# One decoder layer on one core: the tokens of the dilated branch as an even and an odd tile

## The chip, the cores and the metric

The kernel runs on one core of one Trainium2 chip. Its metric is the device time of one execution in microseconds (us); several runs are given by their median. The engines named below are TensorE (PE in the rows, its weight loads PEld), VectorE (DVE), ScalarE (ACT), GpSimd (POOL) and SyncE (SP), which issues most of the DMAs.

## What is computed

A decoder layer with 256 tokens and 2048 channels: `h` is the normalised, modulated input, `proj = h @ w_in` has 20032 columns, and two branches of attention follow, whose gated outputs are projected, merged and projected once more. The change concerns branch B, the dilated attention, with 8 heads of 128 in each of three groups. Every group has its own queries, keys and values, and the outputs of the groups are weighted by their softmax denominators, which equals one softmax over the keys of all three:

```python
DIL_GROUPS = ((128, 1), (512, 4), (2048, 16))      # window, dilation
def dilated_branch(qkv, positions):
    q = partial_rotary(qkv[:, :, 0], positions)     # 32 of the 128 channels of a head are rotated
    k = partial_rotary(qkv[:, :, 1], positions)
    for g, (window, dilation) in enumerate(DIL_GROUPS):
        o, lse = dilated_group_attention(q[:, :, g], k[:, :, g], v[:, :, g], window, dilation)
    wts = jax.nn.softmax(jnp.stack(lses, axis=0), axis=0)
    o = jnp.sum(wts[..., None] * jnp.stack(outs, axis=0), axis=0)
```

A query attends to keys that are not later than itself: in the first group to those at most 128 tokens back, in the second to those whose distance is a multiple of 4, in the third to those whose distance is a multiple of 16.

## The kernel before

**Products with weights.** `load_split` fetches two blocks of 128 rows and 512 columns of a weight, and splits them into a rounded part (`whi`, a cast on ScalarE, L251) and the rest (`wlo`, a subtraction on VectorE, L252). `multiply` then issues 12 matmuls on L262: `hTh` with `whi`, `hTl` with `whi`, `hTh` with `wlo`, each for two blocks of rows and two tiles of 128 tokens. The stationary operand is a 128x128 block of the transposed activations (`Opd.get`), the moving one 512 columns of the weight. For `kva`, the keys' low-rank part, the columns are 256 and 320.

**Stages.** The head of the program alternates the modulation (`ada`, L193) with visits to 16 groups of columns (`head`): nine blocks of queries, keys and values of the dilated heads 0 to 3 (`d...0`), two of the gate `zd`, two of `kva`, three of the heads 4 to 7. In the last round of visits `rotary_tables` is called, and after the visit to `zd0` the rotation of the dilated queries and keys (`dil_rope`) and their attention (`dil_steps(0)`). Six more groups for heads 4 to 7 follow, then `dil_steps(1)`, the latent branch, and the output side.

**Steps beside the products.** Attention is cut into small steps in the list `side`; `run` takes one (`tick`) after each chunk of a product, so that they stand between chunks of 12 matmuls on TensorE. For one dilated head they are: `s1`, transposes of queries and keys into `qk`; `s2`, the scores, one tile of queries after the other, 128 keys for the first tile and 256 for the second in each of three groups, with masked maximum and exponential (`softmax`); `s3`, transposes of the probabilities, nine blocks (`probs_t`); `s4`, nine products with the values, and the gate. A pool framework orders the instructions of every engine; each engine works through its own queue in order. Matmuls on plain float32 operands, such as `s_D` and `pv_D`, leave two records each in the trace; transposes and the products of L262 leave one.

Lines of before that the rows name: L251 and L252 the split, L262 the products, L390 to L399 the angles, L412 and L413 the tables read with a step of two, L421 to L424 the rotation, L474 the masked maximum, L487 the transposes of `s3`, L495 and L496 those of `s1`, L525 the scores, L543 the products with the values, L636 the adding up of a visit's product in SBUF.

Of the kernel before, what the change touches and what calls it, by code (L numbers as in the profile page):

```python
# [49 lines left out]
T_MD0 = T_ZER + P  # L50
T_MD1 = T_MD0 + 3 * P
T_END = T_MD1 + 3 * S


def constant_table():
# [5 lines left out]
    rel0 = np.arange(P)[:, None] - np.arange(P)[None, :]  # L61
    rel1 = P + np.arange(P)[:, None] - np.arange(S)[None, :]

    def masks(rel):
        causal = rel >= 0
        return [causal & (rel <= 128), causal & (rel % 4 == 0), causal & (rel % 16 == 0)]

    t[:, T_MD0:T_MD0 + 3 * P] = np.where(np.concatenate(masks(rel0), 1), 0.0, NEG)
    t[:, T_MD1:T_MD1 + 3 * S] = np.where(np.concatenate(masks(rel1), 1), 0.0, NEG)
# [4 lines left out]
def hybrid_block(ctx: ExitStack, tc: tile.TileContext, x, c, positions, w_ada, b_ada, g_pre, g_post,  # L74
# [225 lines left out]
    for q in range(4):  # L300
# [8 lines left out]
        for t in range(2):  # L309
            j = sp.tile([P, 768], F32, tag="sm", name=f"junk_x{q}{t}")  # L310
# [64 lines left out]
    def rotary_tables():  # L375
        nc.sync.dma_start(msk, table[:, T_ZER:T_END])
        posi = cp.tile([2, P], I32, tag="posi", name="posi")
        nc.sync.dma_start(posi, positions[0].rearrange("(r p) -> r p", p=P))
# [25 lines left out]
        for h in range(2):  # L404
            for d in range(2):
                V.tensor_copy(cosM[:, :, h, d * 32:(d + 1) * 32], cs)
                V.tensor_scalar(sinM[:, :, h, d * 32:(d + 1) * 32], sn, 2.0 * d - 1.0, None, op0=ALU.mult)
        cs2 = cs.rearrange("p t (i two) -> p t i two", two=2)[:, :, :, 0]
        sn2 = sn.rearrange("p t (i two) -> p t i two", two=2)[:, :, :, 0]
# [72 lines left out]
    def probs_t(sm, nb, name):  # L482
        pT = sp.tile([P, 6, P], F32, tag="pT", name=f"pT_{name}")
        for b0 in range(0, nb, 3):
            pt = tp_tile([P, 3, P], f"pt_p{name}{b0}")
            for b in range(3):
                T.transpose(pt[:, b, :], sm[:, (b0 + b) * P:(b0 + b + 1) * P], ident)  # L487
            A.copy(pT[:, b0:b0 + 3, :], pt)
        return pT
# [396 lines left out]
```

## Time and profile before

| | |
|---|---|
| median of 3 runs (lowest to highest) | 1280.65 us (1280.48 to 1281.94) |
| profiled execution, its own time | 1281.44 us |
| its span, first to last instruction | 1279.7 us |
| TensorE busy | 1260.7 us, 99% of the span, 6101 matmul records |
| TensorE's weight loads busy | 1050.0 us, 82% |
| VectorE, ScalarE busy | 814.8 us (64%), 601.9 us (47%) |
| moved by DMA | 275.01 MB, 215 GB/s in the mean |

Busy time of an engine is the time in which one of its instructions is under way. Matmuls are pipelined: a record lasts longer than the distance to the next one. What a matmul takes on the path is therefore the distance of starts, and where many follow one another this is read from the starts of two groups in the timeline.

### The profile page before, as it was taken

What the parts mean: (1) busy time and instruction counts of PE and PEld (TensorE: products, weight loads), DVE (VectorE), ACT (ScalarE), POOL (GpSimd) and SP (SyncE); (2) the same over time, 40 slices, a digit from 0 to 9 for tenths busy, and PEclk for the clock granted to TensorE, in tenths of its full rate; (3) what the DMA queues carried; (4) which work ended last, traced back from release to release, by engine and by line L of the source; (5) the groups of instructions that cost most, each with busy time, mean ns of one, the idle gap of its engine ahead of it and who ended that gap; (6) DMA issues with size and microseconds to landing.
All of it is one profiled execution on the core that took longest, in us unless ns stands there. A gap on an engine that the chain in (4) does not pass through costs nothing.

```text
span 1279.7 us, 16445 instructions
## 1 busy us (share of the span) xinstructions
PE 1260.7 (99%) x6101; PEld 1050.0 (82%) x6101; DVE 814.8 (64%) x1201; ACT 601.9 (47%) x778; POOL 0.2 (0%) x4
## 2 busy tenths in 40 slices
PE   7999999999999999999999999999999999999997
PEld 3788888888888888888888888888888888888886
DVE  4878887897984645556566576664544444565545
ACT  3556334433374544464554555555544444434442
POOL 0000000000000000000000000000000000000000
PEclk9999999999999999999999999999999999999999
DMA  9999988987554566656577585775566666666741
GB/s 329 313 304 334 317 277 281 309 269 233 171 160 119 156 190 195 185 158 215 164 223 243 171 281 175 225 229 161 154 196 196 192 191 196 206 214 187 256 155 67
DMA packets 158172, 275.01 MB, mean 215 GB/s; under 512 B 9542, under 2 KB 46860, under 8 KB 158092
## 3 DMA queue, kind: packets, MB, share of 16 engines
q1 hardware_dynamic: 156276, 268.43, 67.9%
q10 hardware_dynamic: 1816, 5.53, 1.2%
q8 instruction: 48, 0.79, 0.2%
q14 instruction: 32, 0.26, 0.1%
HBM read 271.83 MB, written 2.10 MB: 214 GB/s over the span
## 4 chain that ended last, share of the span: by engine, by line
PE 98%; DVE 1%; DMA 0%; ACT 0%; issue 0%; DVEq 0%; SPq 0%; ACTq 0%
PE acc_d L262 31%; PE acc_mq L262 10%; PE acc_zm L262 7%; PE acc_gd L262 7%; PE acc_ym L262 7%; PE acc_gm L262 7%; PE acc_o L262 6%; PE acc_kv L262 3%; PE acc_yd L262 3%; PE acc_zd L262 3%; PE acc_kva L262 2%; PE pv_D L543 1%; PE s_D L525 1%; PE s_M L722 1%; PE row L186 1%; PE pt_pD L487 1%
## 5 line engine op out<-in xcount | busy, mean ns | idle before, releaser
L251 ACT CAST whi_d<-raw_d 128x1024 fp32r<-128x1024 f32 (+1 forms) x156 | 152.7, 986 | 182.5 <-PE acc_d L262 138.7
L252 DVE TENSOR_TENSOR wlo_d<-raw_d,whi_d 128x1024 fp32r<-128x1024 f32 (+1 forms) x156 | 176.4, 1139 | 72.6 <-ACT whi_d L251 70.9
L262 PE MATMUL acc_d<-whi_d,hTh 128*128 128x512 f32 x576 | 160.2, 396 | 1.4 <-DVE d L636 1.4
L262 PE MATMUL acc_d<-whi_d,hTl 128*128 128x512 f32 x576 | 157.2, 391 | 0.0
L262 PE MATMUL acc_d<-wlo_d,hTh 128*128 128x512 f32 x576 | 156.2, 390 | 0.0
L262 PEld LDWEIGHTS acc_d<-whi_d,hTl 128*128 128x128 f32 x576 | 108.5, 189 | 23.8 <-DVE hTl L229 0.8
L262 PEld LDWEIGHTS acc_d<-wlo_d,hTh 128*128 128x128 f32 x576 | 108.4, 188 | 22.9
L262 PEld LDWEIGHTS acc_d<-whi_d,hTh 128*128 128x128 f32 x576 | 106.3, 188 | 22.7 <-issue 1.8
L252 DVE TENSOR_TENSOR wlo_mq<-raw_mq,whi_mq 128x1024 fp32r<-128x1024 f32 x48 | 58.7, 1223 | 49.4 <-ACT whi_mq L251 44.6
L193 DVE SCALAR_TENSOR_TENSOR ada<-raw_a,ccol,ada 128x512 f32<-128x512 f32 (+1 forms) x96 | 77.4, 807 | 17.1 <-DMA raw_a<-in_w_ada 16.0
L251 ACT CAST whi_mq<-raw_mq 128x1024 fp32r<-128x1024 f32 x48 | 50.4, 1050 | 59.6 <-PE acc_mq L262 26.9
L252 DVE TENSOR_TENSOR wlo_gm<-raw_gm,whi_gm 128x1024 fp32r<-128x1024 f32 x32 | 39.2, 1225 | 45.4 <-ACT whi_gm L251 45.4
L252 DVE TENSOR_TENSOR wlo_gd<-raw_gd,whi_gd 128x1024 fp32r<-128x1024 f32 x32 | 39.2, 1224 | 37.3 <-ACT whi_gd L251 37.3
L252 DVE TENSOR_TENSOR wlo_zm<-raw_zm,whi_zm 128x1024 fp32r<-128x1024 f32 x32 | 39.2, 1224 | 33.5 <-ACT whi_zm L251 27.5
L252 DVE TENSOR_TENSOR wlo_ym<-raw_ym,whi_ym 128x1024 fp32r<-128x1024 f32 x32 | 39.1, 1222 | 32.1 <-ACT whi_ym L251 32.1
L251 ACT CAST whi_ym<-raw_ym 128x1024 fp32r<-128x1024 f32 x32 | 33.7, 1055 | 51.0 <-PE acc_ym L262 41.0
L251 ACT CAST whi_gm<-raw_gm 128x1024 fp32r<-128x1024 f32 x32 | 33.8, 1055 | 49.6 <-PE acc_gm L262 43.9
L252 DVE TENSOR_TENSOR wlo_o<-raw_o,whi_o 128x1024 fp32r<-128x1024 f32 x28 | 34.2, 1224 | 35.4 <-ACT whi_o L251 32.4
L262 PE MATMUL acc_mq<-whi_mq,hTh 128*128 128x512 f32 x192 | 55.2, 409 | 0.0
L251 ACT CAST whi_gd<-raw_gd 128x1024 fp32r<-128x1024 f32 x32 | 33.6, 1051 | 40.9 <-PE acc_gd L262 18.7
L251 ACT CAST whi_zm<-raw_zm 128x1024 fp32r<-128x1024 f32 x32 | 33.6, 1051 | 39.5 <-PE acc_zm L262 12.5
L262 PE MATMUL acc_mq<-whi_mq,hTl 128*128 128x512 f32 x192 | 51.6, 391 | 0.0
(279 smaller groups left out, 2352.2 us busy)
## 6 DMA issues: line engine op xcount, KB each, us to landing
raw_d<-in_w_in SPq DMA_DIRECT2D x132, 512.0 KB, 4.5
raw_mq<-in_w_in SPq DMA_DIRECT2D x48, 512.0 KB, 4.5
raw_a<-in_w_ada SPq DMA_DIRECT2D x80, 256.0 KB, 4.7
raw_zm<-in_w_in SPq DMA_DIRECT2D x32, 512.0 KB, 4.2
raw_g<-in_w_ada SPq DMA_DIRECT2D x32, 512.0 KB, 4.4
raw_gd<-in_w_in SPq DMA_DIRECT2D x32, 512.0 KB, 4.4
raw_gm<-in_w_in SPq DMA_DIRECT2D x32, 512.0 KB, 4.4
raw_ym<-in_w_mla_proj SPq DMA_DIRECT2D x32, 512.0 KB, 3.9
```

The lines of the kernel that those rows point to most:

```text
L186: T.matmul(row[0:1, j, 0:n], ccol[:, kk:kk + 1], v[:, k, j, :], start=kk == ROW_K[0], stop=kk == ROW_K[-1])
L193: V.scalar_tensor_tensor(flat, w, ccol[:, kk:kk + 1], flat, op0=ALU.mult, op1=ALU.add)
L251: A.copy(whi[:, :m], raw[:, :m])
L252: V.tensor_tensor(wlo[:, :m], raw[:, :m], whi[:, :m].bitcast(F32), ALU.subtract)
L262: T.matmul(acc[:, t, :n], opd.get(part, k0 + k, t), wt[:, k * n:(k + 1) * n], start=start and ph == 0 and k == 0, stop=stop and ph == 2 an ...
L487: T.transpose(pt[:, b, :], sm[:, (b0 + b) * P:(b0 + b + 1) * P], ident)
L525: T.matmul(sc[:, i * nk:(i + 1) * nk], qk[g][:, 0, t * P:(t + 1) * P], qk[g][:, 1, 0:nk], start=True, stop=True)
L543: T.matmul(pv, pT[:, b, :], dil[2, g, quad][:, kt, hs], start=b == 0, stop=b == nb - 1)
L722: T.matmul(sc[:, o:o + nk], qk[:, 0, t * P:(t + 1) * P], qk[:, 1, 0:nk], start=True, stop=False)
```

## The change

Tokens of the dilated branch are held as two tiles, the even tokens and the odd ones, instead of the first 128 and the last 128. A distance of 4 or 16 joins only tokens of the same tile, so groups 1 and 2 need one block of 128 keys for each tile of queries; group 0 needs both blocks in either tile. Per head the scores go from three products of 128 keys and three of 256 to two of 256 and four of 128; blocks of probabilities to transpose and to multiply with the values go from nine to eight.

To get there, the products for all dilated columns and for `zd` read `hT` through `hD`: the 128 columns of the stationary operand lie two elements apart. `kva` keeps `hT`. The rotary tables are made for four rows of positions (two in the old order for the latent branch, two even and odd), with a second small DMA that gathers the positions with a step of two. The gated output is written back in the order of tokens, by splits of 128 columns with a step of two. Masks and scratch tiles change their sizes; `sm` goes from two buffers of 768 columns to three of 512.

```diff
+    class OpdDil(Opd):
+        def get(self, part, k, t):
+            return part[k // 4][:, k % 4, :].rearrange("p (m t) -> p t m", t=2)[:, t]
+
     hT = Opd(hT_h, hT_l)
+    hD = OpdDil(hT_h, hT_l)
...
-        posi = cp.tile([2, P], I32, tag="posi", name="posi")
-        nc.sync.dma_start(posi, positions[0].rearrange("(r p) -> r p", p=P))
+        posi = cp.tile([4, P], I32, tag="posi", name="posi")
+        nc.sync.dma_start(posi[0:2], positions[0].rearrange("(r p) -> r p", p=P))
+        nc.sync.dma_start(posi[2:4], positions[0].rearrange("(m t) -> t m", t=2))
...
-        for t in range(2):
+        for t in range(4):
             V.tensor_scalar(ang[:, t, :], frq, posc[:, t:t + 1], None, op0=ALU.mult)
...
-            v = pt.rearrange("p b t n -> p b (t n)")
-            split(dst_h[i][:, 2 * hp:2 * hp + 2, :], dst_l[i][:, 2 * hp:2 * hp + 2, :], v)
+            if dilated:
+                for b in range(2):
+                    hi, lo = [d[i][:, 2 * hp + b, :].rearrange("p (m t) -> p t m", t=2)
+                              for d in (dst_h, dst_l)]
+                    split(hi, lo, pt[:, b])
...
+                sc = tp_tile([P, 4 * P], f"s_D{quad}{h}{t}")
+                own = slice(t * P, (t + 1) * P)
+                T.matmul(sc[:, 0:S], qk[0][:, 0, own], qk[0][:, 1, :], start=True, stop=True)
+                for g in (1, 2):
+                    T.matmul(sc[:, (g + 1) * P:(g + 2) * P], qk[g][:, 0, own], qk[g][:, 1, own],
+                             start=True, stop=True)
+                res.append(softmax(sc, md[t], SC_DIL, f"D{quad}{h}{t}"))
...
-                for b in range(nb):
-                    g, kt = divmod(b, t + 1)
-                    T.matmul(pv, pT[:, b, :], dil[2, g, quad][:, kt, hs], start=b == 0, stop=b == nb - 1)
+                for b, (g, kt) in enumerate(((0, 0), (0, 1), (1, t), (2, t))):
+                    T.matmul(pv, pT[:, b, :], dil[2, g, quad][:, kt, hs], start=b == 0, stop=b == 3)
...
-        run(acc, hT, win, a, upto, c0, n, nm)
+        run(acc, hT if nm.startswith("kva") else hD, win, a, upto, c0, n, nm)
...
-            acc = group(hT, win, KC, dil_col(s, g, 1), 512, nm)
+            acc = group(hD, win, KC, dil_col(s, g, 1), 512, nm)
```

TensorE's queue where the probabilities of the first head are turned (`pt_pD`, step `s3`) and the scores of the second are made (`s_D`, step `s2`); `acc_d` is the product that goes on between them. Before:

```order
L487 MATMUL pt_pD_3281<-tid,sm_D_3200 128x128 x3
L487 MATMUL pt_pD_3287<-tid,sm_D_3211 128x128 x3
L487 MATMUL pt_pD_3292<-tid,sm_D_3211 128x128 x3
L262 MATMUL acc_d_12_3298<-whi_d_12_3301,hTh_2277 128x512 x4
L262 MATMUL acc_d_12_3298<-whi_d_12_3301,hTl_2278 128x512 x4
L262 MATMUL acc_d_12_3298<-wlo_d_12_3302,hTh_2277 128x512 x4
L525 MATMUL s_D_3317<-qkD_3244 128x128
L525 MATMUL s_D_3317<-qkD_3251 128x128
L525 MATMUL s_D_3317<-qkD_3258 128x128
L525 MATMUL s_D_3327<-qkD_3244 128x256
L525 MATMUL s_D_3327<-qkD_3251 128x256
L525 MATMUL s_D_3330<-qkD_3258 128x256
```

The same place now:

```order
L502 MATMUL pt_pD_3282<-tid,sm_D_3203 128x128 x4
L502 MATMUL pt_pD_3289<-tid,sm_D_3213 128x128 x4
L274 MATMUL acc_d_12_3296<-whi_d_12_3299,hTh_2277 128x512 x4
L274 MATMUL acc_d_12_3296<-whi_d_12_3299,hTl_2278 128x512 x4
L274 MATMUL acc_d_12_3296<-wlo_d_12_3300,hTh_2277 128x512 x4
L536 MATMUL s_D_3315<-qkD_3245 128x256
L538 MATMUL s_D_3315<-qkD_3252 128x128
L538 MATMUL s_D_3315<-qkD_3259 128x128
L536 MATMUL s_D_3325<-qkD_3245 128x256
L538 MATMUL s_D_3325<-qkD_3252 128x128
L538 MATMUL s_D_3325<-qkD_3259 128x128
```

One transpose of nine is gone, and one of the three scores against 256 keys has become one against 128; the products around them stand as they stood.

TensorE's queue at the first head, where the rotated queries and keys are turned for the first time (`pt_qkD`, step `s1`; `d_203` and `d_206` are queries and keys of group 1, `d_204` and `d_207` those of group 2) between the products of `kva` and `zd`. Before:

```order
L262 MATMUL acc_kva_14_3177<-whi_kva_14_3180,hTh_2277 128x320 x2
L496 MATMUL pt_qkD_3162<-tid,d_206 128x128
L495 MATMUL pt_qkD_3162<-tid,d_203 128x128
L496 MATMUL pt_qkD_3162<-tid,d_206 128x128
L262 MATMUL acc_kva_14_3177<-whi_kva_14_3180,hTh_2277 128x320 x2
L262 MATMUL acc_kva_14_3177<-whi_kva_14_3180,hTl_2278 128x320 x4
L262 MATMUL acc_kva_14_3177<-wlo_kva_14_3181,hTh_2277 128x320 x4
L525 MATMUL s_D_3196<-qkD_3160 128x128
L525 MATMUL s_D_3196<-qkD_3167 128x128
L525 MATMUL s_D_3206<-qkD_3160 128x256
L525 MATMUL s_D_3206<-qkD_3167 128x256
L496 MATMUL pt_qkD_3169<-tid,d_207 128x128
```

The same place now, after four matmuls of `acc_kva` on `hTh`:

```order
L274 MATMUL acc_kva_14_3180<-whi_kva_14_3183,hTl_2278 128x320 x3
L511 MATMUL pt_qkD_3165<-tid,d_206 128x128
L510 MATMUL pt_qkD_3165<-tid,d_203 128x128
L511 MATMUL pt_qkD_3165<-tid,d_206 128x128
L274 MATMUL acc_kva_14_3180<-whi_kva_14_3183,hTl_2278 128x320
L274 MATMUL acc_kva_14_3180<-wlo_kva_14_3184,hTh_2277 128x320 x4
L536 MATMUL s_D_3199<-qkD_3163 128x256
L538 MATMUL s_D_3199<-qkD_3170 128x128
L536 MATMUL s_D_3209<-qkD_3163 128x256
L538 MATMUL s_D_3209<-qkD_3170 128x128
L274 MATMUL acc_zd_14_3221<-whi_zd_14_3224,hTh_2277 128x512 x2
L511 MATMUL pt_qkD_3172<-tid,d_207 128x128
```

The transposes of `d_206` stand five matmuls of `kva` later than they did, those of `d_207` two matmuls of `zd` later.

VectorE's queue at the same place: the rotation of `d_206` and `d_207` (its last step writes `d_206<-rt_d`) between the splits (`wlo`) and the adding up of visits (`zd`, `kva`). Before:

```order
L252 TENSOR_TENSOR wlo_zd_14_3224<-raw_zd_14_3221,whi_zd_14_3223 128x1024
L636 TENSOR_TENSOR zd_211<-zd_211,acc_zd_14_3079 128x1024
L424 TENSOR_TENSOR d_206<-rt_d_3124,rt_d_3125 128x8x32
L636 TENSOR_TENSOR kva<-kva,acc_kva_14_3136 128x2x256
L421 TENSOR_TENSOR rt_d_3130<-d_207,cosD 128x256
L422 TENSOR_TENSOR rt_d_3131<-d_207,sinD 128x8x16
L423 TENSOR_TENSOR rt_d_3131<-d_207,sinD 128x8x16
L252 TENSOR_TENSOR wlo_d_14_3265<-raw_d_14_3262,whi_d_14_3264 128x1024
L424 TENSOR_TENSOR d_207<-rt_d_3130,rt_d_3131 128x8x32
L636 TENSOR_TENSOR kva<-kva,acc_kva_14_3177 128x2x256
```

The same place now:

```order
L264 TENSOR_TENSOR wlo_zd_14_3225<-raw_zd_14_3222,whi_zd_14_3224 128x1024
L646 TENSOR_TENSOR zd_211<-zd_211,acc_zd_14_3082 128x1024
L435 TENSOR_TENSOR rt_d_3127<-d_206,cosD 128x256
L436 TENSOR_TENSOR rt_d_3128<-d_206,sinD 128x8x16
L437 TENSOR_TENSOR rt_d_3128<-d_206,sinD 128x8x16
L646 TENSOR_TENSOR kva<-kva,acc_kva_14_3139 128x2x256
L438 TENSOR_TENSOR d_206<-rt_d_3127,rt_d_3128 128x8x32
L264 TENSOR_TENSOR wlo_d_14_3266<-raw_d_14_3263,whi_d_14_3265 128x1024
L435 TENSOR_TENSOR rt_d_3133<-d_207,cosD 128x256
L436 TENSOR_TENSOR rt_d_3134<-d_207,sinD 128x8x16
L437 TENSOR_TENSOR rt_d_3134<-d_207,sinD 128x8x16
L646 TENSOR_TENSOR kva<-kva,acc_kva_14_3180 128x2x256
```

The last step of either rotation stands behind the adding up of `kva` that it stood ahead of (that of `d_207` is the row after the last one shown).

## Rows read from the trace of the kernel before

**Rows 1.** The page, chain of work that ended last, by engine:

```profile
PE 98%; DVE 1%; DMA 0%; ACT 0%; issue 0%; DVEq 0%; SPq 0%; ACTq 0%
```

**Rows 2.** Who waited for whom, TensorE: us in total, times, longest:

```profile
PE acc_d L262 <- DVE d L636: 1.4, 1, 1.4
```

**Rows 3.** Timeline of TensorE, dilated steps between chunks: start us, us from first start:

```profile
367.71 1.07 PE L262 MATMUL acc_d<-wlo_d,hTh 128*128 128x512 f32 x4
368.62 1.14 PE L487 MATMUL pt_pD<-tid,sm_D 128*128 128x128 f32 x9
...
370.53 1.08 PE L262 MATMUL acc_d<-whi_d,hTl 128*128 128x512 f32 x4
...
372.36 2.13 PE L525 MATMUL s_D<-qkD 128*128 128x128 f32 x12
...
375.25 1.08 PE L262 MATMUL acc_d<-whi_d,hTl 128*128 128x512 f32 x4
...
377.09 2.17 PE L543 MATMUL pv_D<-d,pT_D 128*128 128x128 f32 x18
...
380.02 1.08 PE L262 MATMUL acc_d<-whi_d,hTl 128*128 128x512 f32 x4
```

**Rows 4.** Groups by line and form, scores: busy us, mean ns | idle before:

```profile
L525 PE MATMUL s_D<-qkD 128*128 128x256 f32 x48 | 11.8, 380 | 0.0
...
L525 PE MATMUL s_D<-qkD 128*128 128x128 f32 x48 | 6.8, 274 | 0.0
```

**Rows 5.** Groups by line, TensorE's weight loads, same columns:

```profile
L262 PEld LDWEIGHTS acc_d<-whi_d,hTl 128*128 128x128 f32 x576 | 108.5, 189 | 23.8 <-DVE hTl L229 0.8
...
L186 PEld LDWEIGHTS row<-raw_a,ccol 128*1 128x1 f32 x36 | 2.8, 83 | 8.1 <-issue 7.2 <-DMA raw_a<-in_w_ada 0.9
```

**Rows 6.** Timeline of the weight loads, the first for the values' products:

```profile
376.86 1.31 PEld L543 LDWEIGHTS pv_D<-d,pT_D 128*128 128x128 f32 x10
```

**Rows 7.** Timeline of VectorE: start us, us, in brackets idle before and releaser:

```profile
328.37 1.23 DVE L252 TENSOR_TENSOR wlo_d<-raw_d,whi_d 128x1024 fp32r<-128x1024 f32 x1 [0.32 <-ACT whi_d L251]
...
330.91 1.22 DVE L636 TENSOR_TENSOR d<-d,acc_d 128x1024 f32<-128x1024 f32 x1 [0.20 <-PE acc_d L262]
...
333.10 0.17 DVE L412 COPY cosD<-cs 128x32 f32<-128x32 f32 x1
...
351.13 0.42 DVE L421 TENSOR_TENSOR rt_d<-d,cosD 128x256 f32<-128x256 f32 x1
...
357.08 0.42 DVE L424 TENSOR_TENSOR d<-rt_d,rt_d 128x256 f32<-128x256 f32 x1
357.42 0.68 DVE L636 TENSOR_TENSOR kva<-kva,acc_kva 128x512 f32<-128x512 f32 x1
...
359.89 0.42 DVE L424 TENSOR_TENSOR d<-rt_d,rt_d 128x256 f32<-128x256 f32 x1
```

**Rows 8.** Windows: us, busy of PE, PEld, DVE, ACT, POOL, clock, DMA share, GB/s:

```profile
331.00:363.00 32.00, 32.00 (x162) 27.24 (x161) 31.90 (x73) 13.59 (x18) 0.00 (x0) 1.00 0.58 172
363.00:420.00 57.00, 57.00 (x326) 49.36 (x325) 32.98 (x77) 34.69 (x55) 0.00 (x0) 1.00 0.47 132
```

**Rows 9.** Timeline of TensorE, first transposes of `d_206` and `d_207`, product of `kva`:

```profile
357.68 0.27 PE L496 MATMUL pt_qkD<-tid,d 128*128 128x128 f32 x1
...
358.30 0.75 PE L262 MATMUL acc_kva<-whi_kva,hTl 128*128 128x320 f32 x4
358.88 0.75 PE L262 MATMUL acc_kva<-wlo_kva,hTh 128*128 128x320 f32 x4
...
360.78 0.27 PE L496 MATMUL pt_qkD<-tid,d 128*128 128x128 f32 x1
```

**Rows 10.** Timeline of SyncE and VectorE, the positions' transfer and its first reader:

```profile
181.78 0.36 SPq L378 DMA_DIRECT2D posi<-in_positions  x1
...
189.70 0.21 DVE L380 CAST posf<-posi 2x128 f32<-2x128 int32 x1
...
194.11 0.75 DVE L193 SCALAR_TENSOR_TENSOR ada<-raw_a,ccol,ada 128x512 f32<-128x512 f32 x1 [2.73 <-DMA raw_a<-in_w_ada]
```

More of the change, by code (lines that the diff above doesn't have):

```diff
@@ L49, with dilated_tokens @@
 T_ZER = T_FRQ + 32
-T_MD0 = T_ZER + P
-T_MD1 = T_MD0 + 3 * P
-T_END = T_MD1 + 3 * S
+T_CAU = T_ZER + P
+T_MD = T_CAU + P
+T_END = T_MD + 2 * 4 * P
+def dilated_tokens(t):
+    return 2 * np.arange(P) + t
 def constant_table():
@@ L60, in constant_table @@
     t[:, T_FRQ:T_FRQ + 32] = inv.astype(np.float32)[None, :]
[L61 to L69, printed above, removed]
+    rel = np.arange(P)[:, None] - np.arange(P)[None, :]
+    t[:, T_CAU:T_CAU + P] = np.where(rel >= 0, 0.0, NEG)
+    for tile_q in range(2):
+        q = dilated_tokens(tile_q)[:, None]
+        rels = [q - dilated_tokens(tile_k)[None, :] for tile_k in (0, 1, tile_q, tile_q)]
+        ok = [(r >= 0) & (r <= 128) for r in rels[:2]]
+        ok += [(rels[2] >= 0) & (rels[2] % 4 == 0), (rels[3] >= 0) & (rels[3] % 16 == 0)]
+        c0 = T_MD + tile_q * 4 * P
+        t[:, c0:c0 + 4 * P] = np.where(np.concatenate(ok, 1), 0.0, NEG)
     return t
@@ L309, in hybrid_block @@
         for t in range(2):
-            j = sp.tile([P, 768], F32, tag="sm", name=f"junk_x{q}{t}")
+            j = sp.tile([P, 512], F32, tag="sm", bufs=3, name=f"junk_x{q}{t}")
             if t == 0:
@@ L405, in rotary_tables @@
             for d in range(2):
[L406 to L409, printed above, removed]
+                V.tensor_copy(cosM[:, :, h, d * 32:(d + 1) * 32], cs[:, 0:2])
+                V.tensor_scalar(sinM[:, :, h, d * 32:(d + 1) * 32], sn[:, 0:2], 2.0 * d - 1.0, None, op0=ALU.mult)
+        cs2 = cs[:, 2:4].rearrange("p t (i two) -> p t i two", two=2)[:, :, :, 0]
+        sn2 = sn[:, 2:4].rearrange("p t (i two) -> p t i two", two=2)[:, :, :, 0]
         for h in range(4):
@@ L450, in transpose_split, with transpose_steps @@
             split(hi[:, 2 * hp:2 * hp + 2, :], lo[:, 2 * hp:2 * hp + 2, :], v)
-    def transpose_steps(src, dst_h, dst_l, i, name):
+    def transpose_steps(src, dst_h, dst_l, i, name, dilated=False):
         def step(hp):
@@ L482, in probs_t @@
     def probs_t(sm, nb, name):
[L483 to L488, printed above, removed]
+        pT = sp.tile([P, 4, P], F32, tag="pT", bufs=2, name=f"pT_{name}")
+        pt = tp_tile([P, nb, P], f"pt_p{name}")
+        for b in range(nb):
+            T.transpose(pt[:, b, :], sm[:, b * P:(b + 1) * P], ident)
+        A.copy(pT[:, 0:nb, :], pt)
         return pT
@@ L499, in qk_t @@
         return qk.rearrange("p (a t) n -> p a (t n)", a=2)
-    md0 = msk[:, P:4 * P]
-    md1 = msk[:, 4 * P:4 * P + 3 * S]
+    md = [msk[:, (2 + 4 * t) * P:(6 + 4 * t) * P] for t in range(2)]
     mm = [msk[:, P:2 * P], msk[:, 0:2 * P]]
@@ L519, in s2 @@
             for t in range(2):
-                nk = (t + 1) * P
-                srcs = []
-                for gs in ((0, 1, 2),) if t == 0 else ((0, 1), (2,)):
-                    sc = tp_tile([P, len(gs) * nk], f"s_D{quad}{h}{t}{gs[0]}")
-                    for i, g in enumerate(gs):
-                        T.matmul(sc[:, i * nk:(i + 1) * nk], qk[g][:, 0, t * P:(t + 1) * P],
-                                 qk[g][:, 1, 0:nk], start=True, stop=True)
-                    srcs.append(sc)
-                res.append(softmax(srcs, md1 if t else md0, 3 * nk, SC_DIL, f"D{quad}{h}{t}"))
+                sc = tp_tile([P, 4 * P], f"s_D{quad}{h}{t}")
[5 more added lines that the diff above has]
+                res.append(softmax(sc, md[t], SC_DIL, f"D{quad}{h}{t}"))
             kept[h] = res
         def s3(h):
-            kept[h] = [(probs_t(sm, 3 * (t + 1), f"D{quad}{h}{t}"), rl) for t, (sm, rl) in enumerate(kept[h])]
+            kept[h] = [(probs_t(sm, 4, f"D{quad}{h}{t}"), rl) for t, (sm, rl) in enumerate(kept[h])]
         def s4(h):
@@ L548, in dil_steps @@
         return ([lambda f=f, h=h: f(h) for f, h in order]
-                + transpose_steps(lambda: bb[0], bbT_h, bbT_l, quad, "bb"))
+                + transpose_steps(lambda: bb[0], bbT_h, bbT_l, quad, "bb", True))
     ckv_h, ckv_l = [], []
```

37 lines of the change are left out of this document (17 added, 20 removed).

## Prediction

> **What bounds the kernel now.** Read the chain of work that ended last first: 98% of it is TensorE [rows 1]. Then ask whether TensorE ever waits in the steady state: the table of who waited for whom has one wait in a product of L262, 1.4 us once [rows 2]. So inside the products the time is what TensorE's queue takes, matmul after matmul, and an edit is worth what it takes out of that queue or puts into it. VectorE, ScalarE and the DMAs matter only where TensorE would come to wait for them.
>
> A record's duration is not that price, since matmuls overlap; the distance of starts is. Four matmuls of 512 columns start in 368.62 - 367.71 = 0.91 us, 0.2275 us each, at the full granted clock [rows 3, 8]. For the small pieces, take the distance between the group and the second group behind it, and take off the four matmuls of 0.91 us between (the first matmul behind a float32 group has its start put too early). Nine transposes: 370.53 - 368.62 - 0.91 = 1.00, 0.111 us each. Eighteen records of the values' products: 380.02 - 377.09 - 0.91 = 2.02, 0.112 each. Twelve records of the scores, six of 128 and six of 256 keys: 375.25 - 372.36 - 0.91 = 1.98; the two forms differ by 380 - 274 = 106 ns a record [rows 3, 4], so a record of 256 keys costs 0.218 and one of 128 costs 0.112.
>
> **What leaves TensorE's queue.** There are eight dilated heads. Per head one score against 256 keys becomes one against 128: two records, 2 x 0.106 = 0.212 us. One product with the values goes: 2 x 0.112 = 0.224. One transpose of probabilities goes: 0.111. Sum 0.547 us a head, **4.4 us** in all. Nothing on TensorE pays for it: the number of scores stays at six a head, and all other transposes and products stay. As TensorE does not wait in these stretches (57.00 busy of 57.00 us in the first of them, with the DMAs at 0.47 [rows 8]), all of it comes off the path. Fewer columns for the maximum, the exponential and the copies are off the path and worth nothing by themselves.
>
> **What the stationary operands cost.** `acc_d` has 3 x 576 matmuls and `zd` 2 groups of 96, so 1920 matmuls get weights that are read with a step of two. This is the unknown that decides: 1 ns each is 1.9 us. No stationary operand of before is read with a step. What the rows tell is how much room a load has. A load of 128 columns lasts 189 ns, one of a single column 83 [rows 5], so 127 columns take 106 ns and the rest is a latency. Loads overlap the matmuls: the first load for the values' products starts at 376.86 and its matmul at 377.09 [rows 3, 6], one matmul of 512 columns earlier; and in the stream of 128 columns one load and one matmul fit into every 0.112 us though a load lasts longer. So a load occupies some 106 to 112 ns of the 227 ns that a matmul of 512 columns takes. If reading with a step doubled it, it would occupy 212 to 224 ns, still under 227. Only a load more than twice as slow comes into the open. The nearest row of a read with a step of two is VectorE's, `cosD<-cs`, 0.17 us for 32 columns [rows 7], too short to show a price. I take **0**; the bounds are 0 and, if the load grew fourfold, 4 x 106 + 7 - 227 = 204 ns each, 392 us. A gain from the step has no mechanism and is left out.
>
> [...]
>
> **The positions' second transfer** is issued two places behind the first, which went out at 181.78; its reader on VectorE's queue ran at 189.70, and behind it VectorE stands idle for 2.73 us before 194.11 [rows 10]. It has 6 us to land, and 2.7 more before it delays anything. Its issue, about the 0.36 us of the first, delays the transfers queued behind it on SP by as much. Cost 0. With that cover gone, the splits behind that reader would come late and TensorE would wait for what exceeds it.
>
> **The rotary tables and the first head** are the one place where a wait can arise. VectorE is busy 31.90 us of the 32 from 331 to 363 [rows 8], so a delay put in ahead of this stretch is still there at its end. Eight operations on the angles double from 64 to 128 columns; from 0.17 us for 32 columns to 0.42 for 256 [rows 7] that is 1.1 ns a column, 0.07 each, 0.57 in all. Two more of 32 columns cost at most 0.17 each: 0.9 at most. Two idle gaps ahead of the stretch, 0.32 and 0.20, can take up to 0.5 of it [rows 7]. I take a delay of 0.5 us. Then the order: the last rotation of `d_206` and of `d_207` now stands behind the adding up of `kva`, about 0.6 us. So `d_206` is ready at 357.08 + 0.5 + 0.6 + 0.42 = 358.6 instead of 357.5. TensorE comes to it five matmuls of `kva` later than at 357.68; one of these takes (358.88 - 358.30) / 4 = 0.145 [rows 9], so at 358.4. A wait of 0.2, with the semaphore 0.3. `d_207`: 359.89 + 1.1 + 0.42 = 361.4, against 360.78 plus two matmuls of 512 columns plus the first wait, 361.5: no second wait. Cost **0.3 us**, between 0 (all of the delay is absorbed) and 1.0 (none is, and the copies of `qk` on ScalarE come late too). Queued behind the waiting transpose is all of TensorE; nothing makes up for it.
>
> The splits of `bb` into four pieces instead of two run on VectorE and ScalarE in stretches where both have slack (32.98 and 34.69 busy of 57 us [rows 8]), and their reader, the product `yd`, comes far later. Cost 0; without that slack it would be some 2 us of VectorE's time. The masks have the same number of columns as before.
>
> **Sum.** -4.4 + 0 + 0.3 = -4.1 us. The profiled execution took 1281.44 us for a span of 1279.7; it would come to 1277.3. It lies 0.8 above the median of 1280.65, from which I forecast **1276.5 us** (-0.32%).
>
> **Rivals.** [...] (b) The load itself more than doubles: threefold is 3 x 106 + 7 - 227 = 98 ns, 1920 x 0.098 = 188 us, **1465 us**. Against it: nothing in the rows is near such a price. (c) Small losses eat the gain: 1 ns a load through rivalry of the wider reads with other reads and writes of SBUF (1.9 us), and 1 us of waiting at the first head instead of 0.3: 1276.5 + 1.9 + 0.7 = **1279.1 us**, no difference. For it: the gain is small, 2.6 us would be lost in many ways, and VectorE at the first head is full. Against it: the price per load has to fall into a narrow band, from about 0.8 to 3.5 ns. (d) That the change does not take out what it says can be ruled out by the order: both queues were counted.
>
> **How the numbers follow.** Forecast 0.64, (c) 0.17, (a) 0.13, (b) 0.06. About 0.2%, 2.6 us, is what a measurement of this kernel can tell from no change. The forecast's own range is 1275 to 1278 (4.4 taken as 5.2, if smaller copies free something, to 1.0 lost at the first head), all of it faster. With (c), 1278 to 1284, the two hold 0.81, and the range is **1274.5 to 1284 us**; (a) and (b) lie beyond. Faster 0.64, same 0.17, slower 0.19.
>
> **What would show it.** Right: in the products of `acc_d` and `acc_zd` groups of four still start 0.91 us apart, as those of `acc_gm` on plain `hT` do; their loads last 188 ns or so, at most 290; TensorE's records fall by 8 + 16 = 24; a wait of some tenths of a microsecond, if any, stands before `pt_qkD` near 358 us, and the distance from the first dilated step to the last one shrinks by the rest. Wrong: starts of `acc_d` 0.24 us apart or more (rival a), or 0.3 and above (b); an idle TensorE of over 1 us at the first head, or at `wlo_kva` near 196 us behind the positions' transfer.

## The result, and the profile after

The changed kernel takes **1290.21 us** (median of 4 runs, 1288.62 to 1290.8) against 1281.3 us of the kernel before in the same rounds (1280.48 to 1282.06): a ratio of 1.0064 [1.0051, 1.0076], slower by about 8 us. The forecast was 1276.5 us and faster. The profiled execution has a span of 1288.3 us at a granted clock of 0.995.

What the change was to take out did go out. Groups by line and form of the changed kernel (line, engine, operation, count | busy us, mean ns of one | idle before):

```profile
L553 PE MATMUL pv_D<-d,pT_D 128*128 128x128 f32 x128 | 15.6, 275 | 0.0
L538 PE MATMUL s_D<-qkD 128*128 128x128 f32 x64 | 9.9, 274 | 0.0
L536 PE MATMUL s_D<-qkD 128*128 128x256 f32 x32 | 9.5, 379 | 0.0
L502 PE MATMUL pt_pD<-tid,sm_D 128*128 128x128 f32 x64 | 8.3, 272 | 0.0
```

Of the 48 records of scores against 256 keys [rows 4] 32 are left, and 64 are of 128; pv_D and pt_pD have 128 and 64 records, 16 and 8 fewer. The page counts 6077 records on TensorE, 24 fewer than the 6101 of before, as forecast:

```profile
PE 1269.0 (99%) x6077; PEld 1058.4 (82%) x6077; DVE 815.0 (63%) x1191; ACT 600.1 (47%) x774; POOL 0.2 (0%) x4
...
PE 98%; DVE 1%; DMA 0%; ACT 0%; issue 0%; DVEq 0%; SPq 0%; ACTq 0%
```

The chain of work (second line) is TensorE's for 98%, as in [rows 1]. So fewer instructions took longer, 1269.0 us busy against 1260.7. Who waited for whom on TensorE has the same one wait in a product as [rows 2], and none at the first head:

```profile
PE acc_d L274 <- DVE d L646: 1.4, 1, 1.4
```

No new wait is in it, and the granted clock is 1.00 here (363 to 420 and 468 to 490 us) as in [rows 8], so the pace must have changed. Timeline of TensorE in the changed kernel (start us, us from first start):

```profile
354.65 1.09 PE L274 MATMUL acc_d<-whi_d,hTl 128*128 128x512 f32 x4
355.58 1.09 PE L274 MATMUL acc_d<-wlo_d,hTh 128*128 128x512 f32 x4
356.51 1.09 PE L274 MATMUL acc_d<-whi_d,hTh 128*128 128x512 f32 x4
```

Four matmuls of `acc_d` start 0.93 us apart; in [rows 3] it was 0.91. Over undisturbed stretches the single starts in the trace, in ns, give 233.3 ns a matmul against 226.7, and 1920 x 6.67 ns are 12.8 us. The weight loads say which products: those of `acc_d`, read with a step, last longer than the 189 ns of [rows 5], those of `acc_gm` on plain `hT` don't:

```profile
L274 PEld LDWEIGHTS acc_d<-whi_d,hTl 128*128 128x128 f32 x576 | 112.2, 195 | 23.6 <-DVE hTl L234 0.8
...
L274 PEld LDWEIGHTS acc_gm<-whi_gm,hTh 128*128 128x128 f32 x128 | 24.0, 188 | 5.0
```

One more view places the loss: the first and the last start of one tile's instructions (count: shortest, middle and longest ns, then start of the first to start of the last, us). From the first `acc_d` to the first `acc_gd` lies everything the change touches. The kernel before:

```profile
L262 PE MATMUL acc_d<-whi_d,hTh x576: 389/389/793, 34.0 to 531.3; 128*128 128x512 f32 x192
...
L262 PE MATMUL acc_gd<-whi_gd,hTh x128: 389/389/481, 858.3 to 987.5; 128*128 128x512 f32 x128
```

The changed kernel:

```profile
L274 PE MATMUL acc_d<-whi_d,hTh x576: 387/394/794, 34.6 to 542.2; 128*128 128x512 f32 x192
...
L274 PE MATMUL acc_gd<-whi_gd,hTh x128: 389/389/481, 867.0 to 996.3; 128*128 128x512 f32 x128
```

858.3 - 34.0 = 824.3 us before, 867.0 - 34.6 = 832.4 after: +8.1. Behind it nothing differs: to the end of the span it is 1279.7 - 858.3 = 421.4 us before and 1288.3 - 867.0 = 421.3 after. The other 0.6 us lie ahead of the first `acc_d`.

### The profile page after: what moved, and what is told of

The parts are those of the page before. It is cut to its first block, busy times and chain, and to the rows that moved or that the text cites. A ratio compares the mean times of both kernels' runs of the same rounds, so it can differ in the third digit from the quotient of the medians.

```text
span 1288.3 us, 16374 instructions
## 1 busy us (share of the span) xinstructions
PE 1269.0 (99%) x6077; PEld 1058.4 (82%) x6077; DVE 815.0 (63%) x1191; ACT 600.1 (47%) x774; POOL 0.2 (0%) x4
## 4 chain that ended last, share of the span: by engine, by line
PE 98%; DVE 1%; DMA 0%; ACT 0%; issue 0%; DVEq 0%; SPq 0%; ACTq 0%
PE acc_d L274 32%; PE acc_mq L274 10%; PE acc_zm L274 7%; PE acc_gd L274 7%; PE acc_ym L274 7%; PE acc_gm L274 7%; PE acc_o L274 6%; PE acc_zd L274 3%; PE acc_kv L274 3%; PE acc_yd L274 3%; PE acc_kva L274 2%; PE pv_D L553 1%; PE s_M L732 1%; PE row L191 1%; PE s_D L538 1%; PE pt_pD L502 1%
## 5 line engine op out<-in xcount | busy, mean ns | idle before, releaser
L274 PE MATMUL acc_d<-whi_d,hTh 128*128 128x512 f32 x576 | 163.3, 401 | 1.4 <-DVE d L646 1.4
L274 PE MATMUL acc_d<-whi_d,hTl 128*128 128x512 f32 x576 | 160.9, 397 | 0.0
L274 PE MATMUL acc_d<-wlo_d,hTh 128*128 128x512 f32 x576 | 160.0, 395 | 0.0
L274 PEld LDWEIGHTS acc_d<-whi_d,hTl 128*128 128x128 f32 x576 | 112.2, 195 | 23.6 <-DVE hTl L234 0.8
L274 PEld LDWEIGHTS acc_d<-wlo_d,hTh 128*128 128x128 f32 x576 | 112.0, 195 | 23.0
L274 PEld LDWEIGHTS acc_d<-whi_d,hTh 128*128 128x128 f32 x576 | 109.8, 195 | 22.8 <-issue 1.8
L263 ACT CAST whi_zm<-raw_zm 128x1024 fp32r<-128x1024 f32 x32 | 33.6, 1051 | 40.1 <-PE acc_zm L274 12.5
```

The lines of the kernel that those rows point to most:

```text
L263: A.copy(whi[:, :m], raw[:, :m])
L274: T.matmul(acc[:, t, :n], opd.get(part, k0 + k, t), wt[:, k * n:(k + 1) * n], start=start and ph == 0 and k == 0, stop=stop and ph == 2 an ...
```

## The experiments

**The change without the step, and the step without the change.** Theory F: the step of two costs each matmul that it feeds 6.7 ns, and the rest of the change does what it should. The first kernel is the changed one with the reading in `OpdDil` put back to runs of 128, so that its tiles hold the old tokens:

```diff
-            return part[k // 4][:, k % 4, :].rearrange("p (m t) -> p t m", t=2)[:, t]
+            return part[k // 4][:, k % 4, t * P:(t + 1) * P]
```

> The changed kernel with one thing undone: the stationary operands of the dilated products are read without a step again (so the dilated branch gets its tokens in the old order and computes another result; all instructions, waits and queues are those of the changed kernel). Theory F: in the changed kernel the products with the step start 233 ns apart instead of 227, 6.7 ns x 1920 = 12.8 us, and that is the whole loss. Then this kernel is back at 227 ns in acc_d and acc_zd and takes 1290.2 - 12.8 = 1277.4 us, faster than before by about the 4.4 us taken out of TensorE's queue less some tenths. Rival Q: the slower starts, or part of the loss, come from something else in the change (VectorE's rotary tables, the positions' second transfer, the buffers of the scratch tiles). Then acc_d stays above 227 ns here and the time lies above 1280 us.

Measured: 1277.35 us (7 runs, 1275.75 to 1280.07) against 1280.71, ratio 0.997 [0.9958, 0.9983]. The pace is back; timeline of TensorE:

```profile
470.82 1.07 PE L274 MATMUL acc_d<-whi_d,hTl 128*128 128x512 f32 x4
471.72 1.07 PE L274 MATMUL acc_d<-wlo_d,hTh 128*128 128x512 f32 x4
472.63 1.07 PE L274 MATMUL acc_d<-whi_d,hTh 128*128 128x512 f32 x4
```

Its first and last starts:

```profile
L274 PE MATMUL acc_d<-whi_d,hTh x576: 387/389/774, 35.1 to 530.4; 128*128 128x512 f32 x192
...
L274 PE MATMUL acc_gd<-whi_gd,hTh x128: 389/389/481, 855.2 to 984.4; 128*128 128x512 f32 x128
```

855.2 - 35.1 = 820.1: 4.2 us less than before, where the prediction's sum for the attention was 4.4. F's time is met; Q falls.

The other half is the kernel before with nothing but the step:

```diff
...
-        run(acc, hT, win, a, upto, c0, n, nm)
+        run(acc, hD, win, a, upto, c0, n, nm)
...
-            acc = group(hT, win, KC, dil_col(s, g, 1), 512, nm)
+            acc = group(hD, win, KC, dil_col(s, g, 1), 512, nm)
```

> The kernel before with the step of two alone: the products of the dilated columns, of zd and also of kva read their stationary operand with a step of two (the tokens come out in another order, so the result is another); nothing else of the change. Theory F (the step costs a fixed 6.7 ns for each load that is read so, whatever the width of the matmul): 1920 matmuls of 512 columns at 233 ns, and kva's 192 matmuls of 256 and 320 columns at 127 and 153 ns instead of 120 and 147; 2112 x 6.7 = 14.1 us, 1281 + 14.1 = 1295 us. Rival C (the wider reads compete with the moving stream for SBUF, so the price grows with the columns that are streamed): 512 columns again at 233, but kva at 256 columns only +3.3 ns and at 320 +4.2. Rival Q (other parts of the change): 227 ns and 1281 us.

Measured: 1293.04 us (4 runs, 1292.97 to 1296.18) against 1280.71, ratio 1.0094 [1.0077, 1.0111]. First and last starts:

```profile
L270 PE MATMUL acc_d<-whi_d,hTh x576: 389/394/774, 35.6 to 545.9; 128*128 128x512 f32 x192
...
L270 PE MATMUL acc_gd<-whi_gd,hTh x128: 389/389/481, 873.0 to 1002.3; 128*128 128x512 f32 x128
```

873.0 - 35.6 = 837.4, 13.1 us over before: 6.8 ns for each of the 1920. Put together, -4.2 + 13.1 = 8.9 against the 8.1 that the change shows in this stretch. But F's mechanism, a fixed piece of every load, does not hold. In this kernel the products of `kva` are read with the step too. Timeline, its 320 columns:

```profile
90.63 0.75 PE L270 MATMUL acc_kva<-whi_kva,hTh 128*128 128x320 f32 x4
91.22 0.75 PE L270 MATMUL acc_kva<-whi_kva,hTl 128*128 128x320 f32 x4
91.81 0.75 PE L270 MATMUL acc_kva<-wlo_kva,hTh 128*128 128x320 f32 x4
92.40 0.75 PE L270 MATMUL acc_kva<-whi_kva,hTh 128*128 128x320 f32 x4
```

Twelve matmuls in 92.40 - 90.63 = 1.77 us, 0.59 per four, and 0.58 without the step [rows 9]. In the trace the distances only alternate between 144 and 149 ns; their mean stays at 146.7. The loads are longer here as well (196 ns). So a longer load alone is not the price. C, which expected 4.2 ns more at these narrower products, is nearer than F with 6.7, but its price isn't there either.

**Other steps.** The kernel before, with the last six dilated products read with steps of 1, 2, 3, 4, 8 and 1:

```diff
...
+            return v[:, a:a + 127 * self.n + 1:self.n]
...
-            acc = group(hT, win, KC, dil_col(s, g, 1), 512, nm)
+            n, word = ((1, "one"), (2, "two"), (3, "three"), (4, "four"), (8, "eight"), (1, "last"))[3 * g - 3 + s]
+            acc = group(OpdStep(hT_h, hT_l, n), win, KC, dil_col(s, g, 1), 512, word)
```

> The kernel before, in which the six products that follow the head (96 matmuls of 512 columns each) read their stationary operand with steps of 1, 2, 3, 4, 8 and 1 elements, over the block itself or over its neighbours (so these products are other ones); their accumulators are named acc_one, acc_two, acc_three, acc_four, acc_eight, acc_last. [...] Rival S (a step other than one costs once, whatever it is): 233 ns for all of 2, 3, 4 and 8.

Measured: 1284.64 us (one run). First and last starts, weight loads and matmuls of the first third of each product:

```profile
L275 PEld LDWEIGHTS acc_two<-whi_two,hTh x32: 193/195/200, 421.8 to 443.7; 128*128 128x128 f32 x32
...
L275 PEld LDWEIGHTS acc_three<-whi_three,hTh x32: 251/252/263, 446.2 to 466.4; 128*128 128x128 f32 x32
L275 PE MATMUL acc_three<-whi_three,hTh x32: 393/394/539, 446.2 to 466.7; 128*128 128x512 f32 x32
...
L275 PEld LDWEIGHTS acc_four<-whi_four,hTh x32: 308/310/311, 468.5 to 489.0; 128*128 128x128 f32 x32
L275 PE MATMUL acc_four<-whi_four,hTh x32: 394/398/401, 468.8 to 489.2; 128*128 128x512 f32 x32
...
L275 PEld LDWEIGHTS acc_eight<-whi_eight,hTh x32: 317/329/333, 491.1 to 512.3; 128*128 128x128 f32 x32
L275 PE MATMUL acc_eight<-whi_eight,hTh x32: 397/406/418, 491.3 to 512.6; 128*128 128x512 f32 x32
...
L275 PEld LDWEIGHTS acc_last<-whi_last,hTh x32: 187/188/202, 514.5 to 534.3; 128*128 128x128 f32 x32
L275 PE MATMUL acc_last<-whi_last,hTh x32: 389/389/400, 514.8 to 534.5; 128*128 128x512 f32 x32
```

From the first to the last start lie 87 matmuls: (489.2 - 468.8) / 87 = 234.5 ns at a step of four, 244.8 at eight, 226.4 at one. As the starts are shown to 0.1 us, these are good to about 1 ns; the same starts in ns give 235.0, 244.2 and 226.9. At three, (466.7 - 446.2) / 87 = 235.6 holds one pause for other work. With pauses left out the mean distance is 233.3 at two and 233.5 at three, where one distance in four is 240 ns and the others are 230 to 232. The loads' durations tell another story: 188, 195, 252, 310, 329 ns.

From two to three the load grows by 57 ns and the pace not at all. So up to a step of three the price is paid once, 6.7 ns, as S has it. At four and eight S misses: 235.0 and 244.2 where it had 233. The load is 122 ns longer than a run's at four and 141 at eight. By the prediction's estimate a load occupies 106 ns as a run, so 228 at four and 247 at eight. That the pace rises because the load grows past the 227 ns of a matmul fits these two steps, but no run tests it by itself.

**The step where the load sets the pace.** In the values' products, float32 with 128 columns, a load fills nearly the whole distance (106 of 112 ns by the prediction's estimate). The kernel before, with eight of the nine stationary operands of each head read with a step of two:

```diff
+                    w = pT[:, b, :]
+                    if b // 2 * 2 + 1 < nb:
+                        two = pT[:, b // 2 * 2:b // 2 * 2 + 2, :].rearrange("p b n -> p (b n)")
+                        w = two.rearrange("p (m t) -> p t m", t=2)[:, b % 2]
-                    T.matmul(pv, pT[:, b, :], dil[2, g, quad][:, kt, hs], start=b == 0, stop=b == nb - 1)
+                    T.matmul(pv, w, dil[2, g, quad][:, kt, hs], start=b == 0, stop=b == nb - 1)
```

> The kernel before, in which 8 of 9 of the dilated products with the values (pv_D, plain float32, 128 columns) read their stationary operand, the transposed probabilities, with a step of two over a pair of blocks (other products, so another result). There a load and a matmul take 112 ns, of which a load needs 106 or so: a stream that a longer load must lengthen. Theory F (a fixed piece of some 6.7 ns per load): pv_D starts 118 to 119 ns apart, its loads last 199 instead of 192 ns. Rival D (the load takes twice as long, mostly hidden behind 512 columns): starts 210 ns apart or more. Rival N (only the rounded float32 of the big products pays): 112 ns.

Measured: 1283.32 us (one run). Timeline of TensorE:

```profile
378.24 2.26 PE L547 MATMUL pv_D<-d,pT_D 128*128 128x128 f32 x18
...
381.27 1.08 PE L262 MATMUL acc_d<-whi_d,hTl 128*128 128x512 f32 x4
```

381.27 - 378.24 - 0.91 = 2.12 us for 18 records against 2.02 in [rows 3]; 0.10 us on 16 stepped records is 6 ns each, and the median distance is 118 ns instead of 112, as F expected; D and N fall. The loads last 196 ns in the median instead of 192. So here 128 columns of plain float32 pay too, 6 ns. That the longer load is itself what shows here is possible, as it nearly fills the distance, but this run does not separate it from the step.

**The width.** Rivals for what was left: the price grows with the columns (G), belongs to 512 columns only (B), stands at every width (F), or stood at the head's narrow products too but was hidden by something at that place (H, with the same times as F here). Two kernels with six widths, without and with the step. The first line shown is new in both; the pair below it is the one line in which they differ:

```diff
...
+            n = (512, 480, 448, 384, 320, 256)[3 * g - 3 + s]
...
-                multiply(acc, hT, whi, wlo, k, kn, n, k == 0, k + kn == KC)
+                multiply(acc, OpdStep(hT_h, hT_l), whi, wlo, k, kn, n, k == 0, k + kn == KC)
```

> The kernel before, with the six dilated products after the head made 512, 480, 448, 384, 320 and 256 columns wide (accumulators acc_w512 to acc_w256, 96 matmuls each), their stationary operands read without a step; the columns that are dropped are filled from the first group's, so its result is another. It is the yardstick for e6_widths_two. All theories: a matmul starts N/2.4 + 13.3 ns after the one before it, as at 512 (226.7), 320 (146.7) and 256 columns (120.0) in the trace of before: 213.3 at 480, 200.0 at 448, 173.3 at 384. 672 columns less in 96 matmuls are 26.9 us: about 1254 us, more where the loads of weights or the attention no longer keep up with the shorter products.

> The same six widths with every stationary operand of these products read with a step of two (its tokens are then the even and the odd ones, so its result is another). In the run with the step alone, a 512-column product cost 6.7 ns more per matmul, but the 256- and 320-column products of the head nothing on average. F (a fixed piece of each load, whatever the width): 6.7 ns more at each width, 233.3, 220.0, 206.7, 180.0, 153.3, 126.7 ns; 3.8 us above e6_widths_one. H (it is the place, not the width: the head's narrow products have something else that hides it): the same as F here. [...] G (the price grows with the columns past 320): about 5.6 ns at 480, 4.4 at 448, 2.2 at 384, none at 320 and 256; about 1.8 us above.

Measured: 1255.65 and 1256.03 us (one run each), 0.4 apart; single runs of the kernel before lie further apart than that, so the distances have to decide. Where the narrow products start, without the step (timeline of TensorE):

```profile
465.31 0.86 PE L269 MATMUL acc_w<-whi_w,hTh 128*128 128x384 f32 x4
...
481.95 0.74 PE L269 MATMUL acc_w<-whi_w,hTh 128*128 128x320 f32 x4
...
496.02 0.64 PE L269 MATMUL acc_w<-whi_w,hTh 128*128 128x256 f32 x4
```

With it:

```profile
465.72 0.87 PE L269 MATMUL acc_w<-whi_w,hTh 128*128 128x384 f32 x4
...
482.37 0.75 PE L269 MATMUL acc_w<-whi_w,hTh 128*128 128x320 f32 x4
...
496.45 0.64 PE L269 MATMUL acc_w<-whi_w,hTh 128*128 128x256 f32 x4
```

A product is 96 matmuls: 16.64 / 96 = 173.3 ns at 384 columns and 14.07 / 96 = 146.6 at 320, against 16.65 and 14.08 with the step. No price; F and H fall, and G too, since 448 and 480 columns, by their distances with pauses left out, pay nothing near its 4.4 and 5.6 ns (202.7 and 203.4; 217.0 and 215.3). But the yardstick itself missed: without any step 448 and 480 columns take 2.7 and 3.7 ns more than the expected N/2.4 + 13.3.

**Where the weights lie.** If not the step alone makes a matmul slower, perhaps the place of the streamed weights does. The price weighed is the step's 6.7 ns: at 512 columns only (B), with weights at a multiple of 2 KB in their buffer (A), or growing with the columns (G). Six products again: 480 columns at a pitch of 512 (from one block of rows to the next in the buffer), 496 and 504 columns at a pitch of as many, and 512 columns that begin 8 or 256 columns into their buffer, or at its start, with and without the step:

```diff
...
+            n, pitch, off, word = ((480, 512, 0, "cut"), (496, 496, 0, "near"), (504, 504, 0, "next"),
+                                   (512, 512, 8, "off"), (512, 512, 256, "half"), (512, 512, 0, "full"))[3 * g - 3 + s]
...
```

> The kernel before, with its six dilated products after the head changed in width and in where the streamed weights lie, stationary operands without a step: acc_cut 480 columns at a pitch of 512, acc_near 496, acc_next 504 columns (the dropped columns filled from the first group's), acc_off and acc_half 512 columns that begin 8 and 256 columns into their buffer (one block of rows per buffer instead of two), acc_full 512 columns as ever. Its result is another. It is the yardstick for e7_place_two. All theories: N/2.4 + 13.3 ns in an undisturbed stretch: 213.3 at 480, 220.0 at 496, 223.3 at 504, 226.7 at 512, wherever the weights lie; where the neighbours disturb, some ns more, as e6_widths_one showed (217.0 at 480, 229.9 at 512).

> The same six products with every stationary operand read with a step of two (other tokens, another result). [...] A (it belongs to weights that lie at a multiple of 2 KB in their buffer against the stationary operand): acc_full pays 6.7 ns and so does acc_cut (480 columns at a pitch of 512), but acc_off and acc_half with their shifted starts pay nothing, nor acc_near and acc_next. G (it grows with the columns): acc_next pays about 6, acc_near about 5, acc_cut about 4 ns, the three of 512 columns 6.7.

Measured: 1279.81 and 1281.7 us (one run each). First and last starts without the step:

```profile
L704 PEld LDWEIGHTS acc_off<-whi_off,hTh x32: 187/187/188, 465.1 to 486.4; 128*128 128x128 f32 x32
L704 PE MATMUL acc_off<-whi_off,hTh x32: 393/395/397, 465.4 to 486.6; 128*128 128x512 f32 x32
...
L704 PE MATMUL acc_half<-whi_half,hTh x32: 389/389/397, 487.8 to 508.4; 128*128 128x512 f32 x32
...
L704 PE MATMUL acc_full<-whi_full,hTh x32: 389/389/389, 509.5 to 529.3; 128*128 128x512 f32 x32
```

With the step:

```profile
L704 PE MATMUL acc_off<-whi_off,hTh x32: 392/396/398, 466.0 to 487.3; 128*128 128x512 f32 x32
...
L704 PE MATMUL acc_half<-whi_half,hTh x32: 392/394/394, 488.4 to 509.6; 128*128 128x512 f32 x32
...
L704 PE MATMUL acc_full<-whi_full,hTh x32: 394/394/394, 510.8 to 531.1; 128*128 128x512 f32 x32
```

Without the step, `acc_off` takes 487.8 - 465.4 = 22.4 us, 233.3 ns a matmul, and `acc_half` 509.5 - 487.8 = 21.7 us, 226 to 227: weights that lie 32 bytes off cost what the step costs, with a load that is as short as ever (187 ns); 1 KB off costs nothing. With the step both take 22.4 us. The two don't add. So A falls, since `acc_half` pays and `acc_cut` does not, and B is right that of these only 512 columns pay, `acc_off` having paid already. But all theories had put the plain matmul at 226.7 ns wherever the weights lie, and that is false: it can lose the same 6.7 ns without any step. The distances of both pairs of kernels, in ns, pauses for other work left out:

| streamed columns | run of 128 | step of two | run, over N/2.4 |
|---|---|---|---|
| 256 | 120.0 | 119.9 | 13.3 |
| 320 | 146.6 | 146.6 | 13.3 |
| 384 | 173.4 | 173.5 | 13.4 |
| 448 | 202.7 | 203.4 | 16.0 |
| 480 | 217.0 | 215.3 | 17.0 |
| 496 | 223.2 | 225.1 | 16.5 |
| 504 | 226.8 | 226.9 | 16.8 |
| 512 | 226.7 | 233.3 | 13.4 |
| 512, 32 bytes off | 233.3 | 233.4 | 20.0 |
| 512, 1 KB off | 227.1 | 233.3 | 13.8 |

The rows of 480 and 496 columns lie in stretches where other work disturbs the pace by some ns (480 columns of this pair of kernels: 216.5 and 216.6), so the 1.9 ns at 496 are not a clear price. N/2.4, 0.417 ns a column, is the slope from 256 to 384 columns, (173.4 - 120.0) / 128. Read down the last column: up to 384 columns a matmul takes 13.3 ns over N/2.4, from 448 to 504 it takes 16 to 17, and 512 columns take either 13.4, in their place with a run, or 20.0. Nor does a shifted place always cost: at 504 columns the second block of rows in a buffer begins 2016 bytes in, 32 short of 2 KB, and its matmuls start 227 ns apart like those of the first.

**A version without a step.** What remains of the change when the loads are runs is worth 3 to 4 us. For that, the even and the odd tokens have to lie in a run each. `hT` is stored as blocks of 64 tokens in the order even and odd of the first half, odd and even of the second, and the first block again: then both plain tiles and both dilated tiles are runs of 128.

```diff
...
-            return part[k // 4][:, k % 4, :].rearrange("p (m t) -> p t m", t=2)[:, t]
+            return part[k // 4][:, k % 4, (192, 64)[t]:(192, 64)[t] + P]
...
+            A.activation(hT_h[q][:, b, S:HP], h[:, 0:64], AF.Identity, bias=colsh[:, k:k + 1])
+            A.copy(hT_l[q][:, b, S:HP], hT_l[q][:, b, 0:64])
...
```

> A version that keeps the change's smaller attention but reads no stationary operand with a step: hT is stored as four blocks of 64 tokens and a copy of the first, even tokens of the first half, odd of the first, odd of the second, even of the second, even of the first again (320 columns, so 1280 bytes from one row of four to the next). The two plain tiles are columns 0 to 128 and 128 to 256, the odd tile 64 to 192, the even tile 192 to 320, each a run of 128. Room for it: 19 plain buffers instead of 27 beside 8 of the larger ones, the scratch buffers sm, qk and qst one fewer each. The order is put in where xT and the row factors are copied out of PSUM and taken out where m is transposed. The rule that only the step costs: acc_d and acc_zd start 226.7 ns apart as before, and the time is that of e1_plain_load, 1277.4 us (ratio to the kernel before 0.997), plus up to 1.5 us for the smaller buffers and the added copies (32 of 64 columns in the head). The rule that any load off its 512-byte place costs (as the streamed weights 32 bytes off did in e7_place_one): 233.3 ns in acc_d and acc_zd as in the changed kernel, about 1290 us; and if the pitch of 1280 bytes costs too, also in acc_zm, acc_mq, acc_gd and acc_gm, 1728 products by 6.7 ns more, about 1301 us.

Measured: 1279.23 us (11 runs, 1277.14 to 1282.17) against 1280.83, ratio 0.9985 [0.9976, 0.9994]: 11 us less than the changed kernel, but only 0.15% less than the one before. That is 0.3 us above the 1277.4 to 1278.9 that the first rule gave; the second rule's 1290 falls. Timeline of TensorE in this kernel:

```profile
470.17 1.07 PE L298 MATMUL acc_d<-whi_d,hTl 128*128 128x512 f32 x4
471.08 1.07 PE L298 MATMUL acc_d<-wlo_d,hTh 128*128 128x512 f32 x4
471.98 1.07 PE L298 MATMUL acc_d<-whi_d,hTh 128*128 128x512 f32 x4
```

Who waited for whom has one row that the others lack:

```profile
PE acc_zd L298 <- ACT whi_zd L287: 1.3, 1, 1.3
```

The pace is (471.98 - 470.17) / 2 = 0.905 us per four, as without a step: a pitch of 1280 bytes and a start 256 or 768 bytes into the row cost nothing. The wait, near 93 us, is 1.3 of the 1.9 us from 1277.35 to 1279.23; the rest is not accounted for, and whether the fewer buffers caused the wait was not separated.

## Why the prediction was wrong

The step that failed is "What the stationary operands cost", which took **0** for 1920 loads. It asked whether a load, even a doubled one, still fits under the 227 ns of a matmul, and it does: the load grew from 189 to 195 ns. The unspoken other half was that a load which fits cannot change the matmul's pace. The runs show that reading it with a step does, though the load's length is not the reason: 6.7 ns each, 12.8 us by the pace, and 12 to 13 us by the kernel with the step alone. That is 3% of a matmul, and 2.3 ns, 1%, would have eaten the whole gain. No row of before could exclude 1%, and 13.3 ns in the trace of before were the sign that something in the matmul's distance was not understood: the line through its 120.0, 146.7 and 226.7 ns at 256, 320 and 512 columns leaves them over at no column.

**Rival (a)**, starts of `acc_d` 0.24 us apart or more, to which the prediction gave 0.13, had the sign and not the size: they stand 233.3 ns apart. From 4.1 / 1920 = 2.1 ns each on, the forecast's gain is gone. Nor does every load pay: at 256 to 384 columns the step costs nothing.

**The range** ended at 1284, where rival (c) ended, and the next case began at starts of 0.24 us, 12.5 ns over the 0.2275 of [rows 3]: 1920 x 12.5 ns = 24 us, so about 1300. A price anywhere between 4 and 12 ns was in no case, though nothing excluded it. Rival (b) did not come, nor would it at a step of four, where the load lasts 310 ns instead of 188 and the pace rises by 8 ns (235.0).

**What held.** The attention's -4.4 us: 4.2 in the kernel with plain loads. TensorE's 24 records. The wait at the first head, forecast at 0.3 us, was smaller than that. The table of waits has none, but in the kernel with plain loads VectorE's last step for `d_206` ends at 359.67, and TensorE turns it at 359.73:

```profile
359.25 0.42 DVE L438 TENSOR_TENSOR d<-rt_d,rt_d 128x256 f32<-128x256 f32 x1
...
359.73 0.33 PE L511 MATMUL pt_qkD<-tid,d 128*128 128x128 f32 x1
```

Around this transpose two distances are 183 and 164 ns where the kernel before has 146 and 109, so some 0.1 us was lost: VectorE was late, and TensorE came there nearly as late. Its end and TensorE's start lie 0.06 us apart; the forecast of this wait had put down 0.1 for the semaphore, an estimate. The positions, VectorE's timeline in the changed kernel:

```profile
193.40 0.74 DVE L198 SCALAR_TENSOR_TENSOR ada<-raw_a,ccol,ada 128x512 f32<-128x512 f32 x1
194.07 0.21 DVE L394 CAST posf<-posi 4x128 f32<-4x128 int32 x1
```

The reader, the second line, runs with no idle time before it, so its data had landed; cost 0. The splits of `bb`: no wait at `acc_yd`; cost 0. The sum with the one term corrected: -4.4 + 12.8 = +8.4, and the change measured +8.1 in its stretch and 8.9 between the medians.

**What stays open** is the mechanism. The runs show which matmuls lose the 6.7 ns (512 columns, with a stepped load or with weights 32 bytes off their place), that the two don't add, and that up to a step of three the load's length is not it. The competition of reads that C named was not shown: at 256 and 320 columns the step costs nothing (119.9 and 146.6 ns), and at 512 the price does not grow with the length of the load from two to three (195 and 252 ns, 233.3 and 233.5). It also stays open why 448 to 504 columns take some 3 ns more than N/2.4 + 13.3 without any step.

## What to carry to other kernels

Before an edit changes how an operand is read in thousands of instructions, work out at which price per instruction it eats the gain; where that is 1% of the instruction's distance, no argument from room or overlap will do, and one product with the new reading tells it. Give a rival's unknown price a range, and let the forecast's range meet it. And if a stationary operand is wanted in another order, pay for it once where it is written, as runs, not at each load.

## What the runs showed of the hardware

The products here stream the two parts of a split weight, rounded and rest, against those of split activations, with a load for each matmul. At the full granted clock (1.00 from 331 to 420 us before and from 468 to 490 in the changed kernel, 0.992 to 0.996 in the mean of each profiled execution), a matmul of 512 such columns starts 226.7 ns after the one before it if its weights lie at the start of their buffer, or 1 or 2 KB into it, and its stationary operand is a run (227.1 at 1 KB), and 233.3 ns if the weights lie 32 bytes in, or if the stationary operand is read with a step of two, or both. From 256 to 384 columns a step of two costs nothing, and the distance is N/2.4 + 13.3 ns (120.0, 146.6 and 173.4); there the place of the weights was not varied. A load of 128 columns lasts 188, 195, 252, 310 and 329 ns at steps of 1, 2, 3, 4 and 8; behind 512 columns the pace is 226.7, 233.3, 233.5, 235.0 and 244.2 ns. In plain float32, where the load nearly fills the distance by the estimate of 106 of 112 ns, a step of two turned 112 ns at 128 columns into 118. The place of the weights and the steps of three and more were measured in one run each.
